# An averaging pool over 16 columns: the last 512 rows cut into nine loads and shared between VectorE and GpSimd

## The chip, the cores and the metric

The kernel runs on one core of one Trainium2 chip. The metric is device time in microseconds (us). Profiles come from one profiled execution each; its span is about 2 us shorter than the timed run (344.62 us timed, 342.5 us of span).

## The reference

```python
# x: float32 [32, 256, 4096], output_size = 256
for i in range(output_size):
    start = int(i * length / output_size)      # 16 * i
    end = int((i + 1) * length / output_size)
    result[:, :, i] = np.mean(x[:, :, start:end], axis=-1)
```

These are 8,192 rows of 4,096 columns. Each row gives 256 means of 16 neighbours. 134.2 MB come in and 8.4 MB go out.

## The kernel before

Each of 31 full tiles holds 256 rows, two per partition (128 x 8,192 values). A tile is loaded through the sync queue, reduced by VectorE, scaled by ScalarE and stored through the scalar queue. The last 256 rows are cut into one load of 128 rows and two half-width loads of 128 rows. Tiles are counted from 0: tile 30 is the last full tile here, and tile 29 is the last full tile of the changed kernel.

```python
R = 2
inpool = ctx.enter_context(tc.tile_pool(name="inpool", bufs=5))
outpool = ctx.enter_context(tc.tile_pool(name="outpool", bufs=5))

def process(row0, r, c0, ncols):
    ...                                               # cut here and below: the tiles and their views
    nc.sync.dma_start(out=tin_v, in_=xin)
    nc.vector.reduce_sum(out=tsum_v, in_=tin_v.rearrange("p (o w) -> p o w", w=window),
                         axis=mybir.AxisListType.X)
    nc.scalar.mul(out=tout_v, in_=tsum_v, mul=inv_w)
    nc.scalar.dma_start(out=out_ap(row0, r, c0, ncols), in_=tout_v)

for i in range(n_main):                               # 31 tiles
    process(row, R, 0, length)
    row += rows_per_main
process(row, 1, 0, length)
row += P
process(row, 1, 0, length // 2)
process(row, 1, length // 2, length // 2)
```

## Time and profile before

| | us | where it is read |
|---|---|---|
| timed run, median of 4 | 344.62 | runs |
| span of the profiled run | 342.5 | page |
| reduce of a full tile | 8.69 | groups by shape |
| distance of full tiles | 10.3 | timeline, starts of the reduces |
| VectorE's work from the last full tile on | 17.4 | timeline |

The page's span and busy times, and its shares of the chain that ended last by engine:

```profile
span 342.5 us, 272 instructions
DVE 278.0 (81%) x34; ACT 21.8 (6%) x35; POOL 0.2 (0%) x4
...
DMA 93%; DVE 4%; DVEq 1%; issue 0%; ACT 0%; SPq 0%
```

VectorE (DVE) is busy for 81% of the span, but the chain runs through transfers. VectorE's timeline at the end has these columns: start, duration, engine, line, operation, output and input, count, and in brackets the idle time before it and what ended that.

```profile
311.84 8.69 DVE L58 TENSOR_REDUCE tsum<-tin 128x512 f32<-128x8192 f32 x1 [1.63 <-DMA tin<-in_x_dram]
322.15 17.40 DVE L58 TENSOR_REDUCE tsum<-tin 128x512 f32<-128x8192 f32 x4 [1.62 <-DMA tin<-in_x_dram]
```

In the steady part a reduce starts every 10.3 us and has waited 1.6 us for its load: transfers set the pace. From 322.15 us VectorE runs four reduces without a gap. There transfers no longer set the pace, and VectorE works off a backlog. The last pieces of the chain in order of time (start, duration, what) are these:

```profile
305.33 24.91 DMA tin<-in_x_dram
...
332.89 4.47 DVEq L109
337.36 2.20 DVE tsum L58
339.56 0.02 issue
339.59 0.31 ACT tout L65
```

The first of these lines is a load that was issued at 305.33 us and landed at 330.24 us. The view of the input tile, cut to the issue near 310 us, shows one more. Its columns are the line, the sync queue's operation, the tiles, the count, the ns that issuing took (min/median/max), and the first and last start in us; the line below has the time from issue to landing.

```profile
L55 SPq DMA_DIRECT2D tin<-in_x_dram x1: 328/328/328, 310.2 to 310.2; - x1
...
DMA to landing us min/median/max: 22.5/22.5/22.5
```

The last load was issued at 310.24 us (timeline of the sync queue) and landed 22.5 us later, at 332.7 us. So 6.8 us of VectorE work (332.74 to 339.56 us) lie behind the last load.

### The profile page before, as it was taken

The numbers are of one execution on the slowest core, as the hardware profiler recorded it, in microseconds if no ns is written. First come the engines' busy times: TensorE is split into PE (matmuls) and PEld (weight loads), VectorE is DVE, ScalarE is ACT, GpSimd is POOL, SyncE is SP. The second block draws the span as 40 slices with busy tenths as digits, with TensorE's granted clock in tenths as the row PEclk, the third lists the DMA queues.
The fourth block names the chain that finished last, engine by engine and source line by source line (L and its number), as shares of the span: only waits on it lengthen the run. The fifth ranks groups of instructions, "written<-read, shape, count | busy, mean of one in ns | idle before, by whom it ended". The sixth has DMA issues, their size and how long they took to land.

```text
span 342.5 us, 272 instructions
## 1 busy us (share of the span) xinstructions
DVE 278.0 (81%) x34; ACT 21.8 (6%) x35; POOL 0.2 (0%) x4
## 2 busy tenths in 40 slices
DVE  0488898888898888988888988887988888988896
ACT  1000000000000000000000000000000000000001
POOL 0000000000000000000000000000000000000000
DMA  8999999999999999999999999999999999999980
GB/s 325 444 432 417 451 419 426 451 406 448 431 415 451 427 422 451 401 445 444 410 451 427 415 455 423 422 448 411 443 439 411 451 423 426 448 415 434 419 344 31
DMA packets 9794, 142.63 MB, mean 416 GB/s; under 512 B 1088, under 2 KB 1472, under 8 KB 5440
## 3 DMA queue, kind: packets, MB, share of 16 engines
q1 hardware_dynamic: 4896, 134.22, 91.0%
q10 hardware_dynamic: 4896, 8.39, 6.4%
q14 instruction: 2, 0.02, 0.0%
HBM read 134.22 MB, written 8.39 MB: 416 GB/s over the span
## 4 chain that ended last, share of the span: by engine, by line
DMA 93%; DVE 4%; DVEq 1%; issue 0%; ACT 0%; SPq 0%
DMA tin<-in_x_dram 89%; DMA out_dram<-tout 4%; DVE tsum L58 4%; DVEq L109 1%; ACT tout L65 0%; SPq L55 0%; DVEq L58 0%
## 5 line engine op out<-in xcount | busy, mean ns | idle before, releaser
L58 DVE TENSOR_REDUCE tsum<-tin 128x512 f32<-128x8192 f32 (+2 forms) x34 | 278.0, 8183 | 61.6 <-DMA tin<-in_x_dram 61.6
L65 ACT ACTIVATE tout<-tsum 128x512 f32<-128x512 f32 (+2 forms) x34 | 20.5, 604 | 317.4 <-DVE tsum L58 317.4
L65 ACT ACT_TABLE_LOAD x1 | 1.3, 1283 | 0.7 <-PEq L95 0.7
L95 POOL MEMSET const-bfloat16-1.0<- 128x1 bf16 x1 | 0.1, 101 | 0.0
L95 POOL MEMSET const-uint8-127<- 128x1 uint8 x1 | 0.1, 101 | 0.0
L95 POOL MEMSET const-float32-0.0<- 128x1 f32 x1 | 0.1, 98 | 0.2 <-issue 0.2
L95 POOL MEMSET const-float32-1.0<- 128x1 f32 x1 | 0.1, 98 | 0.0
## 6 DMA issues: line engine op xcount, KB each, us to landing
tin<-in_x_dram SPq DMA_DIRECT2D x31, 4096.0 KB, 41.2
out_dram<-tout ACTq DMA_DIRECT2D x31, 256.0 KB, 15.0
tin<-in_x_dram SPq DMA_DIRECT2D x1, 2048.0 KB, 36.3
tin<-in_x_dram SPq DMA_DIRECT2D x2, 1024.0 KB, 23.7
out_dram<-tout ACTq DMA_DIRECT2D x1, 128.0 KB, 1.7
out_dram<-tout ACTq DMA_DIRECT2D x2, 64.0 KB, 1.6
```

The lines of the kernel that those rows point to most:

```text
L58: nc.vector.reduce_sum(out=tsum_v, in_=tin_v.rearrange("p (o w) -> p o w", w=window), axis=mybir.AxisListType.X,)
L65: nc.scalar.mul(out=tout_v, in_=tsum_v, mul=inv_w)
L95: nc = _bacc.Bacc("TRN2", target_bir_lowering=False, num_devices=1)
L109: with _tile.TileContext(nc) as tc:
```

## The change

The intent is to shorten what follows the last byte. The last two full tiles' worth of rows (512 rows) become four groups of 128 rows, in nine loads into buffers of their own. GpSimd, idle until then, reduces 6,528 of the 16,384 columns by a tree of pairwise adds. (The recorded prediction says 5,632 and 10,752 for VectorE. That is a slip: its sums, 6,120 elements of adds and 11.4 us of reduces, belong to 6,528 and 9,856.) The stores are moved: the last full tile's store waits behind the last loads, and groups 0 to 2 store through the sync queue. To make room, the input buffers fall from 5 to 3. The core of the diff (asserts, a generic path and pools are cut):

```diff
-    inpool = ctx.enter_context(tc.tile_pool(name="inpool", bufs=5))
-    outpool = ctx.enter_context(tc.tile_pool(name="outpool", bufs=5))
+    inpool = ctx.enter_context(tc.tile_pool(name="inpool", bufs=3))
+    sumpool = ctx.enter_context(tc.tile_pool(name="sumpool", bufs=3))
+    outpool = ctx.enter_context(tc.tile_pool(name="outpool", bufs=3))
 ...
+    def pool_tree(dst, src, name):
+        ...
+        nc.gpsimd.tensor_add(out=s1, in0=src[:, 0:n:2], in1=src[:, 1:n:2])
+        nc.gpsimd.tensor_add(out=s2, in0=s1[:, 0:h1:2], in1=s1[:, 1:h1:2])
+        s3 = s1[:, :h3]
+        nc.gpsimd.tensor_add(out=s3, in0=s2[:, 0:h2:2], in1=s2[:, 1:h2:2])
+        nc.gpsimd.tensor_add(out=dst, in0=s3[:, 0:h3:2], in1=s3[:, 1:h3:2])
 ...
+        if i == nrows // rows_per_main - 3:
+            held = out_ap(row, R, 0, length), tout
+        else:
+            nc.scalar.dma_start(out=out_ap(row, R, 0, length), in_=tout)
 ...
+    # (columns, columns of them that VectorE reduces); GpSimd does the rest
+    groups = [
+        [(4096, 1664)],
+        [(4096, 3072)],
+        [(2048, 1024), (2048, 1024)],
+        [(1536, 1536), (1024, 0), (512, 512), (640, 640), (384, 384)],
+    ]
 ...
+    for g, pieces in enumerate(groups):
 ...
+        for k, (n, dve) in enumerate(pieces):
+            t = g1pool.tile([P, n], fp32, name=f"in{g}_{k}")
+            nc.sync.dma_start(out=t, in_=in_ap(row + g * P, 1, c0, n))
 ...
+    nc.sync.dma_start(out=held[0], in_=held[1])
 ...
+        if dve:
+            dve_reduce(sums[g][:, o:m], t[:, :dve])
+        if dve < n:
+            pool_tree(sums[g][:, m:e], t[:, dve:], "t")
+        if j == len(loaded) - 3:
+            nc.scalar.mul(out=outs[g][:, :o], in_=sums[g][:, :o], mul=inv_w)
+            done = o
+        if c0 + n == length:
+            d = done if g == 3 else 0
+            nc.scalar.mul(out=outs[g][:, d:], in_=sums[g][:, d:], mul=inv_w)
+            eng = nc.scalar if g == 3 else nc.sync
+            eng.dma_start(out=out_ap(row + g * P, 1, 0, length), in_=outs[g])
```

More of the change, by code (lines that the diff above doesn't have):

```diff
@@ L20 @@
     ob, oc, osize = out.shape
+    assert ob == batch and oc == channels
+    assert osize == output_size
     window = length // osize
+    assert window * osize == length, "only integer window supported"
     P = nc.NUM_PARTITIONS
@@ L29 @@
     nrows = xf.shape[0]
-    R = 2
-    inpool = ctx.enter_context(tc.tile_pool(name="inpool", bufs=5))
-    outpool = ctx.enter_context(tc.tile_pool(name="outpool", bufs=5))
+    assert nrows % P == 0
     def in_ap(row0, r, c0, ncols):
@@ L48, in out_ap, with dve_reduce @@
         )
-    def process(row0, r, c0, ncols):
-        og = ncols // window
-        xin = in_ap(row0, r, c0, ncols)
-        tin = inpool.tile([P, R * length], fp32, name="tin")
-        tin_v = tin[:, : r * ncols]
-        nc.sync.dma_start(out=tin_v, in_=xin)
-        tsum = outpool.tile([P, R * osize], fp32, name="tsum")
-        tsum_v = tsum[:, : r * og]
+    def dve_reduce(dst, src):
         nc.vector.reduce_sum(
-            out=tsum_v,
-            in_=tin_v.rearrange("p (o w) -> p o w", w=window),
+            out=dst,
+            in_=src.rearrange("p (o w) -> p o w", w=window),
@@ L61, in process @@
             axis=mybir.AxisListType.X,
         )
-        tout = outpool.tile([P, R * osize], fp32, name="tout")
-        tout_v = tout[:, : r * og]
-        nc.scalar.mul(out=tout_v, in_=tsum_v, mul=inv_w)
-        nc.scalar.dma_start(out=out_ap(row0, r, c0, ncols), in_=tout_v)
+    R = 2
+    FREE = R * length
+    OFREE = R * osize
     rows_per_main = P * R
-    n_main = nrows // rows_per_main - 1
-    row = 0
-    for i in range(n_main):
-        process(row, R, 0, length)
-        row += rows_per_main
@@ L74, with process_simple @@
-    process(row, 1, 0, length)
-    row += P
-    process(row, 1, 0, length // 2)
-    process(row, 1, length // 2, length // 2)
-    row += P
+    generic = not (length == 4096 and window == 16 and nrows % rows_per_main == 0
+                   and nrows // rows_per_main >= 4)
+    inpool = ctx.enter_context(tc.tile_pool(name="inpool", bufs=3))
+    sumpool = ctx.enter_context(tc.tile_pool(name="sumpool", bufs=3))
+    outpool = ctx.enter_context(tc.tile_pool(name="outpool", bufs=3))
+    def process_simple(row0, r, c0, ncols):
+        free = r * ncols
+        og = free // window
+        tin = inpool.tile([P, FREE], fp32, name="tin")[:, :free]
+        nc.sync.dma_start(out=tin, in_=in_ap(row0, r, c0, ncols))
+        tsum = sumpool.tile([P, OFREE], fp32, name="tsum")[:, :og]
+        dve_reduce(tsum, tin)
+        tout = outpool.tile([P, OFREE], fp32, name="tout")[:, :og]
+        nc.scalar.mul(out=tout, in_=tsum, mul=inv_w)
+        nc.scalar.dma_start(out=out_ap(row0, r, c0, ncols), in_=tout)
@@ new lines @@
+    if generic:
+        n_main = nrows // rows_per_main
+        row = 0
+        for i in range(n_main):
+            process_simple(row, R, 0, length)
+            row += rows_per_main
+        rem = nrows - row
+        if rem:
+            assert rem % P == 0
+            process_simple(row, rem // P, 0, length)
+        return
+    s1pool = ctx.enter_context(tc.tile_pool(name="s1pool", bufs=2))
+    s2pool = ctx.enter_context(tc.tile_pool(name="s2pool", bufs=2))
+    g1pool = ctx.enter_context(tc.tile_pool(name="g1pool", bufs=1))
@@ new lines @@
+    g2pool = ctx.enter_context(tc.tile_pool(name="g2pool", bufs=3))
+    tspool = ctx.enter_context(tc.tile_pool(name="tspool", bufs=1))
+    topool = ctx.enter_context(tc.tile_pool(name="topool", bufs=1))
+    S1MAX = 1536
+    S2MAX = 768
+    def pool_tree(dst, src, name):
+        n = src.shape[-1]
+        h1, h2, h3 = n // 2, n // 4, n // 8
+        s1 = s1pool.tile([P, S1MAX], fp32, name="s1")[:, :h1]
+        s2 = s2pool.tile([P, S2MAX], fp32, name="s2")[:, :h2]
+        nc.gpsimd.tensor_add(out=s1, in0=src[:, 0:n:2], in1=src[:, 1:n:2])
[3 more added lines that the diff above has]
+        nc.gpsimd.tensor_add(out=dst, in0=s3[:, 0:h3:2], in1=s3[:, 1:h3:2])
@@ new lines @@
+    row = 0
+    for i in range(nrows // rows_per_main - 2):
+        tin = inpool.tile([P, FREE], fp32, name="tin")
+        nc.sync.dma_start(out=tin, in_=in_ap(row, R, 0, length))
+        tsum = sumpool.tile([P, OFREE], fp32, name="tsum")
+        tout = outpool.tile([P, OFREE], fp32, name="tout")
+        dve_reduce(tsum, tin)
+        nc.scalar.mul(out=tout, in_=tsum, mul=inv_w)
+        if i == nrows // rows_per_main - 3:
+            held = out_ap(row, R, 0, length), tout
+        else:
+            nc.scalar.dma_start(out=out_ap(row, R, 0, length), in_=tout)
+        row += rows_per_main
@@ new lines @@
+    groups = [
[4 more added lines that the diff above has]
+    ]
+    loaded = []
+    for g, pieces in enumerate(groups):
+        c0 = 0
+        for k, (n, dve) in enumerate(pieces):
+            t = g1pool.tile([P, n], fp32, name=f"in{g}_{k}")
+            nc.sync.dma_start(out=t, in_=in_ap(row + g * P, 1, c0, n))
+            loaded.append((g, c0, n, dve, t))
+            c0 += n
@@ new lines @@
+    nc.sync.dma_start(out=held[0], in_=held[1])
+    sums = [tspool.tile([P, osize], fp32, name=f"sum{g}") for g in range(4)]
+    outs = [topool.tile([P, osize], fp32, name=f"out{g}") for g in range(4)]
+    for j, (g, c0, n, dve, t) in enumerate(loaded):
+        o, m, e = c0 // window, (c0 + dve) // window, (c0 + n) // window
+        if dve:
[10 more added lines that the diff above has]
+            eng.dma_start(out=out_ap(row + g * P, 1, 0, length), in_=outs[g])
```

## The prediction

> **What bounds the kernel now.** The page: 342.5 us of span, VectorE 81% busy, a chain that is 93% DMA. From 40 to 290 us the windows view has the DMA engines at share 1.00 and 431 GB/s; VectorE reduces a 128x8192 tile in 8.69 us, then idles 1.6 us for the next load. The steady period of 10.3 us is set by transfers. The end is different: the last full tile is on hand at 322.15 us, from there VectorE runs 17.4 us without a gap (four reduces) to 339.56 us, while the last load landed at 330.24 us (chain in order of time). Then come a 0.31 us scaling, a store and about 2.6 us to the end. Some 9 us of VectorE work lie behind the last byte; only that is to be won.
>
> **What the change does.**
> 1. The last 512 rows become nine loads into buffers of their own. VectorE reduces 10,752 of their 16,384 columns, GpSimd the other 5,632 by four pairwise adds each.
> 2. Input buffers fall from 5 to 3.
> 3. The last full tile's store is held back behind the last loads; three groups store on the sync queue, the last one by one 128 KB store.
>
> **Steady part: nothing.** A load waits for the reduce three tiles back, which ends 8.7 us after that tile's landing, while 1.6 us of the next tile and a whole further one (10.3 us) are queued: transfers do not starve. Tile 29 should be on hand at 311.84 us as before, reduced at 320.53 us.
>
> **The end, VectorE.** From the groups by form (8.686, 4.409, 2.275 us) I estimate 0.14 us + 1.04 ns per column: eight reduces are 11.4 us, less about 0.6 us of overlap between neighbours. VectorE is done at 331.4 us instead of 339.56. The loads should have landed by 329.6 to 330.2 us, so it waits little.
>
> **The end, GpSimd.** No trace shows such an add. The Trainium skill, "GPSIMD Engine Reference", section 3.1, gives 4,497 ns for an fp32 add of 2,048 elements, about 2.2 ns each. The 20 adds write 6,120 elements; with 0.1 to 0.15 us each for semaphores the estimate is 15 to 16.3 us. The first starts when group 0 lands, near 317 us: GpSimd ends at 332 to 333.3 us and is the likelier last one, as the last scaling waits behind its piece in ScalarE's order. The same skill, "SBUF — State Buffer", section "Who interferes with whom", says that a VectorE reduce never contends with GpSimd, so I add nothing.
>
> **Sum.** Last compute 331.5 to 333; scaling 0.3 to 0.7; store and end about 2.8: span 334.6 to 336.7. The timed run is 2 us above the span: about 337.1 us, 7.5 us less than 344.62 (2.2%). Range 335.6 to 339.4. Chances: faster by over 2% 0.6, within 2% 0.37, slower 0.03.
>
> **What would show each step.** Reduces still 10.3 us apart with 1.6 us idle and DMA share 1.00 (buffers cost nothing). VectorE nearly gapless from 311.8 to 331.4 us. GpSimd busy 14 to 16 us in all, its 128x512 add 1.1 to 1.3 us. Last load landing near 330 us. The chain ending in GpSimd or VectorE, a scaling and a store of under 2 us.
>
> **What would make it wrong.** GpSimd adds much dearer than estimated (half as much again: an end near 340 us, the gain gone), or slowing VectorE's reduces; gaps between loads with three buffers; late loads waiting on earlier stores' completions (stores took 15 us to land beside loads); the held and moved stores delaying the last one.

## The result, and the profile after

The changed kernel takes 339.02 us (median of 8 runs, 338.8 to 339.33) against 344.64 us (13 runs). The ratio is 0.9838, with a 95% interval of 0.9829 to 0.9848. That is 1.6% faster. It lies within the predicted range of 335.6 to 339.4 us, but 1.9 us above the central value: 5.6 of the forecast 7.5 us were won, and the result is on the other side of the 2% mark that was given the better chance. The page's busy times and chain after:

```profile
span 337.2 us, 306 instructions
DVE 271.8 (81%) x38; ACT 21.9 (6%) x36; POOL 14.0 (4%) x24
...
DMA 72%; DVE 26%; POOL 1%; issue 0%; ACT 0%; POOLq 0%; DVEq 0%
```

The 26% of VectorE in this chain are not a new limit. With three input buffers a load is issued when the reduce three tiles back ends, so the walk back passes through that reduce; the pace of the reduces did not change. VectorE's timeline at the end of the changed kernel:

```profile
311.91 8.69 DVE L51 TENSOR_REDUCE tsum<-tin 128x512 f32<-128x8192 f32 x1 [1.63 <-DMA tin<-in_x_dram]
320.51 1.88 DVE L51 TENSOR_REDUCE sum<-in 128x104 f32<-128x1664 f32 x1
322.79 4.48 DVE L51 TENSOR_REDUCE sum<-in 128x192 f32<-128x3072 f32 x2 [0.40 <-DMA in<-in_x_dram]
327.76 1.22 DVE L51 TENSOR_REDUCE sum<-in 128x64 f32<-128x1024 f32 x1 [0.49 <-DMA in<-in_x_dram]
329.65 1.75 DVE L51 TENSOR_REDUCE sum<-in 128x96 f32<-128x1536 f32 x1 [0.67 <-DMA in<-in_x_dram]
331.61 2.06 DVE L51 TENSOR_REDUCE sum<-in 128x32 f32<-128x512 f32 x3 [0.21 <-DMA in<-in_x_dram]
```

Tile 29 is on hand at 311.91 us (311.84 before) after the same wait of 1.63 us. After it VectorE waits four times for a load, 1.8 us in all, and ends at 333.67 us (331.61 + 2.06). The last load (the view of the group tiles, cut to its issue) explains this:

```profile
L140 SPq DMA_DIRECT2D in<-in_x_dram x1: 431/431/431, 321.3 to 321.3; - x1
...
DMA to landing us min/median/max: 11.6/11.6/11.6
```

It was issued at 321.3 us and landed at 332.9 us. Before, the last load landed at 332.7 us. The change did not bring the last load forward; it removed nearly all of the work behind it (0.8 us instead of 6.8 us until VectorE's end). GpSimd's groups by shape (busy time and mean ns of one, then the idle time before):

```profile
L107 POOL TENSOR_TENSOR s<-in 128x512 f32<-128x512 f32 x4 | 4.2, 1038 | 0.9 <-DMA in<-in_x_dram 0.9
L107 POOL TENSOR_TENSOR s<-in 128x1216 f32<-128x1216 f32 x1 | 2.2, 2211 | 317.2 <-DMA in<-in_x_dram 317.2
```

The adds are cheaper than estimated: (2,211 - 1,038) ns over 704 elements is 1.67 ns an element, plus some 0.18 us for each instruction. The Trainium skill, "GPSIMD Engine Reference", section 3.1, gives 4,497 ns for 2,048 elements, which is 2.2 ns each. The measurement decides here. The end of the chain in order of time:

```profile
313.87 17.03 DMA in<-in_x_dram
330.90 0.07 issue
330.97 1.05 POOL s L107
...
333.22 0.34 POOLq L190
...
333.82 0.27 ACT out L157
```

GpSimd's last piece of 1,024 columns came at 330.9 us, and its four adds end at 333.54 us, level with VectorE's 333.67 us. Then follow the last scaling, to 334.09 us, and the last store, to the end at 337.2 us.

### The profile page after: what moved, and what is told of

Its sections match the earlier page's. It is cut to its first block, busy times and chain, and to the rows that moved or that the text cites. A ratio compares the mean times of both kernels' runs of the same rounds, so it can differ in the third digit from the quotient of the medians. Undisturbed runs are those within 1.5% of the kernel's fastest.

```text
span 337.2 us, 306 instructions
## 1 busy us (share of the span) xinstructions
DVE 271.8 (81%) x38; ACT 21.9 (6%) x36; POOL 14.0 (4%) x24
## 2 busy tenths in 40 slices
DMA packets 10515, 142.64 MB, mean 423 GB/s; under 512 B 1168, under 2 KB 1808, under 8 KB 6160
## 4 chain that ended last, share of the span: by engine, by line
DMA 72%; DVE 26%; POOL 1%; issue 0%; ACT 0%; POOLq 0%; DVEq 0%
DMA tin<-in_x_dram 63%; DVE tsum L51 26%; DMA in<-in_x_dram 5%; DMA out_dram<-tout 4%; POOL s L107 0%; ACT tout L120 0%; POOL s L108 0%; POOL s L110 0%; POOLq L190 0%; ACT out L157 0%; DVEq L51 0%; ACT out L153 0%
## 5 line engine op out<-in xcount | busy, mean ns | idle before, releaser
L51 DVE TENSOR_REDUCE tsum<-tin 128x512 f32<-128x8192 f32 x30 | 260.6, 8686 | 60.0 <-DMA tin<-in_x_dram 60.0
L120 ACT ACTIVATE tout<-tsum 128x512 f32<-128x512 f32 x30 | 18.9, 629 | 300.4 <-DVE tsum L51 300.4
L107 POOL TENSOR_TENSOR s<-in 128x512 f32<-128x512 f32 (+1 forms) x5 | 6.4, 1273 | 318.1 <-DMA in<-in_x_dram 318.1
L51 DVE TENSOR_REDUCE sum<-in 128x64 f32<-128x1024 f32 (+6 forms) x8 | 11.3, 1432 | 1.9 <-DMA in<-in_x_dram 1.8
L108 POOL TENSOR_TENSOR s<-s 128x256 f32<-128x256 f32 (+1 forms) x5 | 3.6, 729 | 0.4
L110 POOL TENSOR_TENSOR s<-s 128x128 f32<-128x128 f32 (+1 forms) x5 | 2.3, 457 | 0.4
L157 ACT ACTIVATE out<-sum 128x256 f32<-128x256 f32 (+1 forms) x4 | 1.5, 379 | 8.4 <-POOL sum L111 5.1
L111 POOL TENSOR_TENSOR sum<-s 128x64 f32<-128x64 f32 (+1 forms) x5 | 1.6, 321 | 0.4
## 6 DMA issues: line engine op xcount, KB each, us to landing
in<-in_x_dram SPq DMA_DIRECT2D x1, 320.0 KB, 11.4
```

The costliest lines, as they stand in the source:

```text
L51: nc.vector.reduce_sum(out=dst, in_=src.rearrange("p (o w) -> p o w", w=window), axis=mybir.AxisListType.X,)
L107: nc.gpsimd.tensor_add(out=s1, in0=src[:, 0:n:2], in1=src[:, 1:n:2])
L108: nc.gpsimd.tensor_add(out=s2, in0=s1[:, 0:h1:2], in1=s1[:, 1:h1:2])
L110: nc.gpsimd.tensor_add(out=s3, in0=s2[:, 0:h2:2], in1=s2[:, 1:h2:2])
L111: nc.gpsimd.tensor_add(out=dst, in0=s3[:, 0:h3:2], in1=s3[:, 1:h3:2])
L120: nc.scalar.mul(out=tout, in_=tsum, mul=inv_w)
```

## The experiments

Three readings were open. Does the buffer count, GpSimd or something else stand between 339.0 and the predicted 337.1 us? Is the end now bound by the engines that compute or by those that transfer? And why did the last load not come earlier, although 0.26 MB of stores were put behind it? All results were correct unless said otherwise.

### Only the buffers (bufs3)

```diff
 # the kernel before
-    inpool = ... bufs=5
-    outpool = ... bufs=5
+    inpool = ... bufs=3
+    outpool = ... bufs=3
```

> The kernel before with 3 input and 3 output buffers instead of 5, nothing else. Theory (about 12 us of queued transfers remain, so buffers cost nothing): within 0.2% of before, 344.6 us, steady reduces 10.3 us apart. Rival (fewer buffers cost transfers, and the tail's gain had to pay for it, which is why the gain fell short): over 1 us slower than before.

Measured: 344.29 us against 344.54, ratio 0.9993 (0.9978 to 1.0008). Three buffers cost nothing, as predicted, and the buffers are no part of the gain. The trace shows more. The last load and VectorE's end in this run (the view of the input tile cut to the issue near 331 us, then VectorE's line of the timeline):

```profile
L55 SPq DMA_DIRECT2D tin<-in_x_dram x1: 328/328/328, 330.8 to 330.8; - x1
...
DMA to landing us min/median/max: 5.3/5.3/5.3
...
322.07 17.40 DVE L58 TENSOR_REDUCE tsum<-tin 128x512 f32<-128x8192 f32 x4 [1.65 <-DMA tin<-in_x_dram]
```

With three buffers the last load waits until a buffer is free and lands at 336.1 us, over 3 us later than with five. VectorE still runs its 17.4 us without a gap, and the time is the same. So in the kernel before, the landing of the last load does not set the end. The end is set by the landing of tile 30 and the 17.4 us of VectorE work that start there.

### VectorE alone on the finer loads (all_vector)

```diff
-        [(4096, 1664)],
-        [(4096, 3072)],
-        [(2048, 1024), (2048, 1024)],
-        [(1536, 1536), (1024, 0), (512, 512), (640, 640), (384, 384)],
+        [(4096, 4096)],
+        [(4096, 4096)],
+        [(2048, 2048), (2048, 2048)],
+        [(1536, 1536), (1024, 1024), (512, 512), (640, 640), (384, 384)],
```

> The changed kernel with every column of the last 512 rows reduced by VectorE, GpSimd out. Theory (before, the end is VectorE's backlog, and GpSimd's share is the gain): VectorE works from 320.5 us for about 17.5 us to 338 us, span about 341.3, time about 343.2 us (0.4% under before). Rival (the finer loads and the held store give the gain): it stays within 1 us of the changed kernel, 339 us.

Measured: 342.80 us, ratio to before 0.9950 (0.9936 to 0.9965). VectorE's timeline of this run:

```profile
311.75 8.69 DVE L51 TENSOR_REDUCE tsum<-tin 128x512 f32<-128x8192 f32 x1 [1.63 <-DMA tin<-in_x_dram]
320.36 17.69 DVE L51 TENSOR_REDUCE sum<-in 128x256 f32<-128x4096 f32 x9
```

VectorE's backlog is still 17.7 us, now without the wait of 1.6 us that stood before tile 30, because a group of 128 rows is on hand before tile 29 is reduced. Theory and measurement agree (343.2 us expected). So without GpSimd's share the change is worth 0.5%, and with it 1.1% more. The 1,024-column reduce takes 1,214 ns in this run without GpSimd, and 1,214 ns in the changed kernel beside it. That agrees with the Trainium skill, "SBUF — State Buffer", section "Who interferes with whom", by which a VectorE reduce never contends with GpSimd on this chip.

### The last full tile's store not held back (no_hold)

```diff
-        if i == nrows // rows_per_main - 3:
-            held = out_ap(row, R, 0, length), tout
-        else:
+        if True:
             nc.scalar.dma_start(out=out_ap(row, R, 0, length), in_=tout)
 ...
-    nc.sync.dma_start(out=held[0], in_=held[1])
```

> The changed kernel with the store of the last full tile issued at once on the scalar queue. Theory (the end is now bound by transfers, the store's 0.26 MB is 0.61 us at 431 GB/s and runs ahead of the last load): last load lands 0.6 us later, time 339.6 us (+0.18%). Rival (the last compute or the final store's own latency binds): within 0.1 us of the changed kernel.

Measured: 339.65 us, ratio to before 0.9858 (0.9842 to 0.9875). Beside the changed kernel's 0.9838 and 0.9840 this is 0.6 to 0.7 us more, at the expected size; the intervals overlap. It was run at another time. The last load landed at 333.3 us (issue at 322.6 us and 10.7 us), 0.4 us later than in the changed kernel. The same direction is confirmed with a larger step by the next run.

### Four stores held back (hold4)

```diff
-    outpool = ctx.enter_context(tc.tile_pool(name="outpool", bufs=3))
+    outpool = ctx.enter_context(tc.tile_pool(name="outpool", bufs=6))
 ...
-        if i == nrows // rows_per_main - 3:
-            held = out_ap(row, R, 0, length), tout
+        if i >= nrows // rows_per_main - 2 - 4:
+            held.append((out_ap(row, R, 0, length), tout))
 ...
-    nc.sync.dma_start(out=held[0], in_=held[1])
+    for dst, src in held:
+        nc.sync.dma_start(out=dst, in_=src)
```

> The changed kernel with the stores of the last four full tiles held behind the last loads instead of one. Theory (transfers of bytes ahead of the last load bind the end): the last load lands 3 x 0.61 = 1.8 us earlier, and the stores then run while the last pieces are computed; time 337.4 to 338 us, the final store a little delayed by the held ones. Rival (GpSimd and VectorE bind the end: they have little idle time there): less than 0.4 us gained.

Measured: 337.62 us, ratio to before 0.9799 (0.9784 to 0.9814): 2.0% under the kernel before and 0.4% under the changed one. It beats both. The last load and the last compute came earlier by what the three stores' bytes take:

```profile
L141 SPq DMA_DIRECT2D in<-in_x_dram x1: 328/328/328, 316.1 to 316.1; - x1
...
DMA to landing us min/median/max: 14.9/14.9/14.9
```

That is a landing at 331.0 us, 1.9 us before the changed kernel's 332.9; 3 x 0.61 = 1.8 us were expected. Of these, 1.3 us arrive at the end of the span (335.9 us against 337.2). The windows view shows why not all of it. Its columns are the window, its length, the busy times of VectorE, ScalarE and GpSimd with counts, the clock, the DMA share and GB/s. The changed kernel first:

```profile
332.00:333.00 1.00, 0.90 (x2) 0.00 (x0) 0.84 (x3) 1.00 1.05 377
333.00:334.00 1.00, 0.68 (x2) 0.42 (x2) 0.47 (x2) 1.00 0.35 120
334.00:335.00 1.00, 0.00 (x0) 0.09 (x1) 0.00 (x0) 1.00 0.06 16
335.00:336.00 1.00, 0.00 (x0) 0.00 (x0) 0.00 (x0) 1.00 0.36 124
```

The same with four stores held:

```profile
331.00:332.00 1.00, 0.88 (x2) 0.21 (x1) 0.68 (x2) 1.00 1.05 404
332.00:333.00 1.00, 0.00 (x0) 0.30 (x2) 0.00 (x0) 1.00 1.07 383
333.00:334.00 1.00, 0.00 (x0) 0.00 (x0) 0.00 (x0) 1.00 0.83 284
334.00:335.00 1.00, 0.00 (x0) 0.00 (x0) 0.00 (x0) 1.00 0.06 19
```

In the changed kernel the transfers thin out from 333 us on and then move almost nothing until the last 128 KB. With four held, they run through the last compute and on to 334 us, and the last store shares them (2.6 us to land instead of 2.2).

### Six stores held back (hold6)

```diff
 # against four held
-    sumpool = ... bufs=3
-    outpool = ... bufs=6
-    if i >= ... - 2 - 4:
+    sumpool = ... bufs=2
+    outpool = ... bufs=8
+    if i >= ... - 2 - 6:
```

> The stores of the last six full tiles held instead of one (and 2 sum buffers instead of 3, for room). Theory (the engines that transfer are already busy to within a microsecond of the end with four held): no more gain, 337.4 to 337.9 us, because the held stores now run past the last compute and delay the final store. Rival (each held store gives its 0.61 us): 336.5 us or less.

Measured: 337.81 us, ratio to before 0.9801 (0.9788 to 0.9814), the same as with four. The last scaling now ends at 331.27 us, but the last store takes 3.6 us to land beside the held ones. Here holding paid until the held bytes filled the time of the last compute.

### The changed kernel again, and GpSimd nearly free (after_again, pool_free)

```diff
-        nc.gpsimd.tensor_add(out=s1, in0=src[:, 0:n:2], in1=src[:, 1:n:2])
-        ... (the three further adds)
+        # wrong result on purpose: one short add instead of the tree
+        nc.gpsimd.tensor_add(out=dst, in0=src[:, 0:h3:2], in1=src[:, 1:h3:2])
```

> The changed kernel once more, as the yardstick on this chip for the three runs beside it. Ratio to before 0.983 to 0.985, 338.8 to 339.3 us.

> The changed kernel with GpSimd's four adds per piece cut to one short add (wrong result on purpose). Theory (arrivals bind the end; GpSimd is at most level with VectorE): VectorE's last reduce still ends near 333.6 us, gain at most 0.3 us over the changed kernel. Rival (GpSimd, which was estimated as the last engine, is what costs): gain of 0.6 us or more.

Measured: the changed kernel again 339.16 us, ratio 0.9840 (0.9826 to 0.9853); with GpSimd's work cut from about 14 to 1.6 us (one add of 0.44 and four of 0.29 us; result wrong) 339.10 us, ratio 0.9838 (0.9824 to 0.9851). Nothing is gained. The end of its timeline:

```profile
331.63 2.06 DVE L51 TENSOR_REDUCE sum<-in 128x32 f32<-128x512 f32 x3 [0.22 <-DMA in<-in_x_dram]
333.72 0.28 ACT L154 ACTIVATE out<-sum 128x96 f32<-128x96 f32 x1 [1.88 <-DVE sum L51]
```

VectorE's last reduces start and end where they did, behind their loads. GpSimd stands last in the chain, but it is only level with VectorE, and both follow the loads.

### Two large loads at the end (big_last)

```diff
-        [(1536, 1536), (1024, 0), (512, 512), (640, 640), (384, 384)],
+        [(2048, 1024), (2048, 1536)],
 ...
-        if j == len(loaded) - 3:
+        if j == len(loaded) - 1:
```

> The changed kernel with the last group as two loads of 2,048 columns (VectorE 1,024 and 1,536 of them, GpSimd the rest) instead of five loads of 1,536 to 384. Theory (short rows of 1.5 to 2.5 KB lower the transfer rate at the end from 431 to about 390 GB/s, which ate what the held store gave): the windows between 329 and 332 us show 415 GB/s or more and the last load lands 0.3 to 0.5 us earlier, about 332.5 us; the longer last reduce (about 1.75 us) and GpSimd's last 512 columns still make the kernel slower, by 0.8 to 1.3 us. Rival (the row length does not matter): the rate stays near 390 and the last load lands at 332.9 us or later.

Measured: 339.71 us, ratio 0.9858 (0.9844 to 0.9871), 0.6 us slower than the changed kernel, less than expected. The rate in the windows 329:330 and 330:331 us rose to 442 and 434 GB/s, where it was 402 and 390 GB/s in the changed kernel, but in 331:332 us it fell to 359, where it was 398. Over all three it is 412 against 397 GB/s, short of the 415 that was expected. So the larger rows move the rate up only a little. The last load landed at 333.0 us (issue at 314.0 us and 19.0 us), and not at 332.5. The expectation failed on both numbers: short rows do not explain by themselves why the last load came no earlier.

### Groups 0 and 1 in one 4 MB load (one_4mb)

```diff
+        if g < 2:
+            # groups 0 and 1 come in one load of two rows per partition
+            if g == 0:
+                both = g1pool.tile([P, FREE], fp32, name="both")
+                nc.sync.dma_start(out=both, in_=in_ap(row, 2, 0, length))
+            n, dve = pieces[0]
+            loaded.append((g, 0, n, dve, both[:, g * length : (g + 1) * length]))
+            continue
```

The stores of these two groups were adapted to the row order (cut).

> The changed kernel with groups 0 and 1 loaded by one 4 MB load (two rows of 16 KB per partition, so 32 KB runs as in the full tiles) instead of two 2 MB loads. Question: group 1 came 10.8 us after tile 29, where the kernel before had its next full tile after 10.3 us, and the last load came no earlier although a store was held back. Theory (the shorter runs of the loads let the stores beside them take a larger share, so loads fall behind): the 4 MB load lands 10.3 us after tile 29, near 322.2 us, and the last load near 332.4 us. Rival (the time is lost later, among the smallest loads or to stores on engines that finish first): the last load still lands at 332.8 to 333.0 us. In both, GpSimd can only start near 322.3 us and needs 14.7 us, so it ends near 337 us and the kernel is about 3.5 us slower than the changed one, 342.5 us.

Measured: 341.68 us, ratio 0.9917 (0.9900 to 0.9934). The 4 MB load landed at 322.5 us (issue at 289.9 us and 32.6 us), 10.7 us after the start of tile 29's reduce at 311.78 us, not after 10.3 us, and the last load at 332.8 us (323.7 us and 9.1 us). By these landings the theory of the shorter runs falls, and it is the rival's number; a closer reading of the marks behind the landings (under "What stays open") gives the theory a part of it back. The run also shows what the split of this load is worth: GpSimd starts at 322.59 instead of 317.69 us, and the kernel is 0.8% slower than the changed one.

## Why the prediction was right or wrong

- **"Steady part: nothing" was right.** Reduces stay 10.3 us apart with 1.63 us of idle time, and three buffers alone measure 0.9993.
- **"VectorE is done at 331.4 us" was wrong by 2.3 us, and this is the step that made the sum too small.** The prediction took 330.24 us, the landing of the load in the chain of waits, for the landing of the last load. That load was the last but one: the last landed at 332.7 us before. From the wrong number came "the loads should have landed by 329.6 to 330.2 us, so it waits little". They landed until 332.9 us, and VectorE waited 1.8 us of the 2.3. The other 0.5 us is the overlap of neighbours: 0.6 us were taken off the 11.4 us of the eight reduces, but they measured 11.3 us, so the reduces were sized well and hardly overlapped. In the same way "some 9 us of VectorE work lie behind the last byte" was 6.8 us, so there was less to win.
- **"GpSimd ends at 332 to 333.3 us and is the likelier last one": nearly right.** It ended at 333.54 us, level with VectorE. Its adds were cheaper than estimated (13.9 us busy, 15.0 us with the 0.08 us between them, where 15 to 16.3 were estimated; the 128x512 add 1.04 us, under the stated 1.1 to 1.3), but it started at 317.69 instead of 317 us and waited 0.9 us for loads, the last time until 330.9 us. That its work costs nothing here was shown by cutting it to 1.6 us without effect.
- **"Scaling 0.3 to 0.7; store and end about 2.8" was right for the scaling (0.42 us after VectorE) and 0.3 us short for the rest.** From the end of the last scaling, at 334.09 us, to the end of the span were 3.1 us; the store took 2.2 us to land, not under 2 us. What delays it is not shown. Of the 16 completion marks that the trace keeps for this store, 15 came by 335.92 us and one at 336.34 us.
- **The late loads did wait for earlier stores, without harm.** The waits of the sync queue list 28.0 us in four waits of the group loads for stores, but the last load was still issued 11.6 us before it landed, and the transfer engines stayed busy (share 0.97 to 1.07 in every microsecond from 328 to 333 us).
- **Sum.** Last compute at 333.67 us instead of 331.5 to 333, and a store 0.3 us longer, make the span 337.2 us instead of 334.6 to 336.7.
- **What stays open.** Holding a store back moves the last load forward (0.4 us for one, 1.9 us for three more), yet the changed kernel with one held has its last load no earlier than the kernel before with none. About half a microsecond is lost. The views show landings alone, but the packed trace keeps 16 completion marks for each transfer, which we take for one from each transfer engine; a landing is the last of them. The figures that follow were read from these marks, counted from tile 29's load.
  - *By the mean of the 16 marks*, the last load comes after 21.02 us in the kernel before, 21.40 us with no store held and 20.78 us in the changed kernel. So the held store gives 0.62 us, the size expected, and the finer loads cost 0.38 us. Nearly all of this cost is there at group 1: 10.66 us, against 10.32 us for tile 30 before. With one 4 MB load it is 10.39 us. So two 2 MB loads do come later than one of 4 MB; why is not shown. Larger last rows (big_last) bring the last load to 20.59 us, 0.19 us earlier.
  - *The slowest mark* hides part of this. It comes 0.45 us behind the mean for the last load before, and 0.74 us in the changed kernel. There the lag grows from 0.47 us at tile 29's load to 0.84 us at group 0's. An instruction fetch of 8 KB (queue 14 in the DMA view) starts between the two, at 316.26 us; in the kernel before none starts near the end until 331.74 us. That the fetch holds one engine up is a guess: no run moves it, and in pool_free, which has it at 316.27 us, the lag was 0.70 us before it and 0.86 us after it.
  - *The bytes* agree that some engines are done before the slowest: by 333.0 us 142.38 MB had moved (142.64 in all less the 0.26 MB of the windows after it), 0.56 MB more than all loads and the 29 earlier stores. The held store's first mark comes at 332.36 us, before the last mark of the last load at 332.87 us.

## What to carry to other kernels

Where transfers set the pace, an end is shortened in two ways: leave little compute behind the last byte (smaller last pieces, a second engine), and move bytes that nobody waits for, such as earlier stores, behind the last load; the second gave another 0.4% here for a few lines. First ask what sets the end: with three buffers the last load of the kernel before came over 3 us later and the time stayed the same. When you size such a change, find the landing of the last load from its own issue and time to landing, not from the chain of waits, which shows only the loads that happened to be links of it. After the change, check which resource is busy until the end: when the transfers run through the last compute, as with four stores held, more of the same gives nothing.

## What the Trainium skill lacked or had wrong

- "GPSIMD Engine Reference", section 3.1: an fp32 add of 2,048 elements is given as 4,497 ns (2.2 ns an element). Here adds with inputs of step 2 took 1,038 ns for 512 and 2,211 ns for 1,216 elements: 1.67 ns an element and about 0.18 us for each instruction. No run here adds 2,048 elements or inputs of step 1, so the two were not measured alike.
- "DMA: Bandwidth & Descriptors", section "Queues, rings and completion order" (under arbitration), says that an engine takes turns between its queues by packets, but not what this means for a small store beside large loads: a 256 KB store took 15.0 us to land beside full-tile loads, and 10.0 us for the last one that was not held, beside the finer loads.
- The same page has no table of rates by row length for plain loads of this chip: here 431 GB/s with runs of 32 KB in the steady part, stores included, and 397 GB/s between 329 and 332 us with the short rows at the end, against 412 GB/s with rows of 8 KB there.
- No page that was read says that a chain of waits can leave out the last load; the chain before showed a landing at 330.24 us, where the last load landed at 332.7 us.
